# Reordering the first loads of a fused mixer kernel: modulation weights and projection weights ahead of x, two small vectors on another queue

## The chip, the cores and the metric

The kernel runs on one core of a Trainium2 chip. The metric is the device time of one execution in microseconds (us). The kernel before took 438.06 us, the median of three runs (437.89 to 438.6 us). Times inside an execution come from a hardware trace of one profiled execution; all of them are counted from the start of that execution's span.

The engines that appear below are PE (TensorE, matrix multiplications, with PEld for its weight loads), DVE (VectorE), ACT (ScalarE), POOL (GpSimd) and SP (SyncE, which here does nothing but issue DMA transfers).

## What is computed

One inference step of a mixer layer on 640 tokens of width 1024: 128 context tokens and 512 latent tokens. Each group has its own conditioning vector, from which a modulation (shift, scale, gate) is computed; both groups pass through the same weights. Cut to what matters here:

```python
mod   = silu(c) @ w_ada + b_ada              # (3*1024), once for context, once for latent
shift, scale, gate = split(mod, 3)
h     = rmsnorm(x, g_pre) * (1 + scale) + shift
proj  = h @ w_in                             # 1024 x 3840
qa, ka, va, ga, qr, zf, zb, ir, gr, uf, gf = split_columns(proj)
# three branches: neighbourhood attention, bidirectional gated recurrence, Fourier mixing,
# each multiplied by the SiLU of its gate columns
mixed = concat(oa * silu(ga), o_r * silu(gr), o_f * silu(gf))
y     = x + gate * rmsnorm(mixed @ w_out, g_post)
```

The modulated, normalised input h is needed by every projection, so nothing of the three branches can start before the first part of h is there. The outputs are y for both groups, the context keys and values, and the final recurrence states.

## The kernel before, in words

**Data layout.** The width of 1024 is cut into 8 row blocks of 128 (index k). h is kept transposed: for each k a 128x640 tile, feature on the partition, token along the row. Products that need more than the precision of one pass are split: a matrix is written as hi + lo (`hT_105`/`hT_106` for h, `hi`/`lo` for weights), and three passes hi·hi, lo·hi and hi·lo are added in PSUM (`mm3`).

**The start stage** (`start_stream`, `zf_stream`). The following happens for each k:

1. Two 512 KB blocks of modulation weights (`wss`, tiles named `vs` and `pT`) are multiplied with the silu of the conditioning vectors (`csil`): eight 32-column matmuls each (`mod_cols`). Here this is called modulation k, with halves a and b.
2. DVE copies the result from PSUM to `row`; four matmuls with the constant `sel` sum the partial rows (named sel k below); DVE makes G and shift for this k (lines 269 to 271 of the profile).
3. PE transposes the 128 columns of x that belong to k, one 128x128 block for each of the five token blocks i (`txa_107` to `txa_111` hold columns 0 to 639, `txb_112` to `txb_116` the rest), into PSUM. ACT applies G and shift while reading it (`modulated`, L235 for the four latent blocks, L237 for the context block), DVE writes the hi part (L238) and the lo part (L239) of hT.
4. The first projection (`zf`, two weight blocks zf0 and zf1, tiles `raw`, split by ACT into hi at L127 and by DVE into lo at L128) takes twelve 128x320 matmuls for each k, accumulated in four PSUM banks (`pb_117` to `pb_120`).

x itself comes as ten transfers (`load_x`), five token blocks of 320 KB + 192 KB. Before the transposes, `scale_x` takes for each token block the sum of squares (ACT Square at L223, DVE at L224), the reciprocal root (L161, L162, L226) and scales x in place (DVE, L228 and L229).

**What sets the order.** An object `Order` keeps a model clock `od.now` and lets several generators take turns by due times; the order in which they emit instructions is refined by a scheduler with its own timing. Each engine then executes its list in order and waits on semaphores. All large loads are issued by SP, one after the other in program order (`load_raw`, `load`); at most eight transfers are outstanding, since each new one reuses the completion semaphore of the eighth before it and waits for it. POOL issues three small loads (`bss`, `gpre`, `sel`). `cc` (8 KB, the conditioning vectors) and `lbl` (2 KB) are the first two transfers on SP's queue.

**After the start stage** come the other projection blocks (`block`), recurrences, attention, Fourier mixing and the output projection, all fed by weights that SP loads two blocks ahead into the two `raw` buffers.

Of the kernel before, what the change touches and what calls it, by code (L numbers as in the profile page):

```python
# [19 lines left out]
KT = 8  # L20
# [8 lines left out]
EARLY = 3  # L29
# [42 lines left out]
def mixer_kernel(ctx: ExitStack, tc: tile.TileContext, A, O):  # L72
    nc = tc.nc
    sc, ve, gp, te, sy = nc.scalar, nc.vector, nc.gpsimd, nc.tensor, nc.sync
# [8 lines left out]
    od = Order()  # L83
# [3 lines left out]
    def nm(s):  # L87
        n_[0] += 1
        return f"{s}_{n_[0]}"

    def T(cols=NT, dt=F32, tag=""):
        return tp.tile([P, NT], dt, tag="t", name=nm("t" + tag))[:, :cols]

    def PE_():
        return tp.tile([P, 512], F32, tag="pe", name=nm("pe"), bufs=WB["pe"])

    def S(cols):
        if cols <= 16:
            return sp.tile([P, 16], F32, tag="s", name=nm("s"))[:, :cols]
        return sp.tile([P, 320], F32, tag="m", name=nm("m"), bufs=WB["m"])[:, :cols]  # L100
# [4 lines left out]
    def PB(tag="b"):  # L105
        return ps.tile([P, 512], F32, tag=tag, name=nm("pb"), bufs=WB["p" + tag])
# [3 lines left out]
    def mm(out, lhsT, rhs, start=True, stop=True):  # L110
        n, m = rhs.free_size(), lhsT.free_size()
        od.now += 1e-3 * (n * 0.4167 * 4 if rhs.dtype == F32 else max(n * 0.4167, m * 0.83)) + 2e-3
        return te.matmul(out, lhsT, rhs, start=start, stop=stop).ins  # L113
# [8 lines left out]
    def tr(out, src):  # L122
        od.now += 0.107
        last_tr[0] = te.transpose(out, src, ident).ins  # L124

    def split(src, hi, lo, hi_eng=None, lo_eng=None):
        (sc.copy if hi_eng is None else hi_eng.tensor_copy)(hi, src)  # L127
        (ve if lo_eng is None else lo_eng).tensor_sub(lo, src, hi.bitcast(F32))  # L128
# [5 lines left out]
    def const(name, shape, dt=F32, dma=gp.dma_start):  # L134
        t = cp.tile([P, *shape], dt, tag=name, name=name)
        if name in A:
            dma(t, A[name])
        return t

    cc = const("cc", [KT, 2], dma=sy.dma_start)  # L140
    lbl = const("lbl", [2, 2], dma=sy.dma_start)
    bss = const("bss", [KT, 2])
    gpre = const("gpre", [KT])
    sel = const("sel", [2, P])
# [14 lines left out]
    def rsqrt_mean(ss, n):  # L159

        sc.activation(ss, ss, ACT.Sqrt, bias=eps, scale=1.0 / n)  # L161
        ve.reciprocal(ss, ss)  # L162
# [9 lines left out]
    def load_raw(src, tag, shape=(KT, P)):  # L172
        t = (tp if tag == "vs" else wp).tile([P, *shape], F32, tag=tag, name=nm(tag), bufs=WB[tag])
        with tc.issue_after(wdma[-1]) if wdma else ExitStack():
            wdma.append(sy.dma_start(t, src).ins)
        return t

    def split_w(raw, lo_eng=None, shape=(KT, P), tags=("hi", "lo")):
        hi, lo = [wp.tile([P, *shape], F32R, tag=t, name=nm(t), bufs=WB[t]) for t in tags]
        split(raw, hi, lo, lo_eng=lo_eng)  # L180
        return hi, lo
# [5 lines left out]
    def load(t, src):  # L187

        with tc.issue_after(wdma[-1]) if wdma else ExitStack():
            sy.dma_start(t, src)  # L190

    def mod_cols(out, w):

        t = od.now
        for k in range(KT):
            o = out[32 * (k % 4):32 * (k % 4) + 32, :]
            mm(o, csil[:, k, :], w[:, k, :], start=(k < 4), stop=(k >= 4))
        od.now = t + 0.45
# [5 lines left out]
    def xcols(i, k):  # L204
        return (xa[i] if k < 5 else xb[i])[:, k % 5 * P:k % 5 * P + P]
    zf_w, zf_acc = [], [[PB("f"), PB("f")], [PB("f"), PB()]]
# [8 lines left out]
    def load_x():  # L215
        for i in range(5):
            load(xa[i], A["x"][i * P:(i + 1) * P, 0:NT])
            load(xb[i], A["x"][i * P:(i + 1) * P, NT:D])

    def scale_x():  # L220
        for i in range(5):
            ss2 = S(2)
            sc.activation(T(), xa[i], ACT.Square, accum_out=ss2[:, 0:1])  # L223
            ve.tensor_tensor_reduce(PE_()[:, 0:384], xb[i], xb[i], 1.0, 0.0, op0=ALU.mult, op1=ALU.add,  # L224
                                    accum_out=ss2[:, 1:2])
            ve.tensor_add(rstd[:, i:i + 1], ss2[:, 0:1], ss2[:, 1:2])  # L226
            rsqrt_mean(rstd[:, i:i + 1], D)
            ve.tensor_scalar(xa[i], xa[i], rstd[:, i:i + 1], 0.0, op0=ALU.mult, op1=ALU.add)  # L228
            ve.tensor_scalar(xb[i], xb[i], rstd[:, i:i + 1], 0.0, op0=ALU.mult, op1=ALU.add)  # L229

    def modulated(k, pm):
        h, px = T(), PB()
        for i in range(1, 5):
            tr(px[:, (i - 1) * P:i * P], xcols(i, k))
        sc.activation(h[:, P:NT], px, ACT.Identity, bias=shift[:, k, 1:2], scale=G[:, k, 1:2])  # L235
        tr(pm[:, 384:512], xcols(0, k))
        sc.activation(h[:, 0:P], pm[:, 384:512], ACT.Identity, bias=shift[:, k, 0:1], scale=G[:, k, 0:1])  # L237
        ve.tensor_copy(hT[0][:, k, :], h)  # L238
        ve.tensor_sub(hT[1][:, k, :], h, hT[0][:, k, :].bitcast(F32))  # L239
        od.set(f"h{k}", LAT["h"])  # L240

    def start_stream():
        load_x()
        raws, zraw = [], []

        def loads(k):
            for u in range(2):
                raws.append(load_raw(A["wss"][2 * k + u], RAW[2 * k + u]))
            if k < 2:
                zraw.append(load_raw(A["win"][k], "raw"))  # L250

        for k in range(EARLY):
            loads(k)
        scale_x()
        od.now = 11.0
        for k in range(KT):
            if k + EARLY < KT:
                loads(k + EARLY)
            row = sp.tile([P, 256], F32, tag="AC", name=nm("row"), bufs=2)
            pm = PB()  # L260
            for u in range(2):
                mod_cols(pm[:, u * P:(u + 1) * P], raws[2 * k + u])
            yield 0
            ve.tensor_copy(row, pm[:, 0:256])
            yield LAT["row"]
            pt = pm[:, 256:260]
            for u in range(2):
                mm(pt[:, u * 2:u * 2 + 2], row[:, u * P:(u + 1) * P], sel[:, :, 0:1].rearrange("p a b -> p (a b)"))
            ve.tensor_scalar(G[:, k, :], pt[:, 0:2], bss[:, k, 0:1], 1.0, op0=ALU.add, op1=ALU.add)
            ve.tensor_scalar_mul(G[:, k, :], G[:, k, :], gpre[:, k:k + 1])  # L270
            ve.tensor_scalar_add(shift[:, k, :], pt[:, 2:4], bss[:, k, 1:2])
            modulated(k, pm)
            if k < 2:
                zf_w.append(split_w(zraw[k]))
            if k == 1:
                od.set("zw", 0.0)
            yield max(0.0, 13.5 + 2.7 * (k + 1) - od.now)

    def zf_stream():
        yield "zw"  # L280
# [9 lines left out]
        od.set("zf", 0.0)  # L290

    od.add(start_stream())
    od.add(zf_stream())

# [834 lines left out]
```

## Time and profile before

| | |
|---|---|
| time before, median of 3 runs | 438.06 us (437.89 to 438.6) |
| the profiled execution, its own time | 439.14 us |
| its span, first to last instruction | 437.3 us |
| PE busy in the span | 413.5 us, 95% |
| DVE / ACT busy | 302.3 us, 69% / 205.1 us, 47% |
| read from HBM / written | 43.80 MB / 3.28 MB |

The profile page gives the busy time of each engine, the span in 40 slices, and the chain of work that ended last, followed back from the last instruction to the first. The trace can be asked for instructions in order of time, for the same chain piece by piece, for the busy time of each engine in chosen windows, and for single tiles with the time from a DMA's issue to its landing. Matmul ends are modelled, so a busy PE is not always a PE at its peak rate; the distance from start to start is the better price.

### The profile page before, as it was taken

What the parts mean: (1) busy time and instruction counts of PE and PEld (TensorE: products, weight loads), DVE (VectorE), ACT (ScalarE), POOL (GpSimd) and SP (SyncE); (2) the same over time, 40 slices, a digit from 0 to 9 for tenths busy, and PEclk for the clock granted to TensorE, in tenths of its full rate; (3) what the DMA queues carried; (4) which work ended last, traced back from release to release, by engine and by line L of the source; (5) the groups of instructions that cost most, each with busy time, mean ns of one, the idle gap of its engine ahead of it and who ended that gap; (6) DMA issues with size and microseconds to landing.
All of it is one profiled execution on the core that took longest, in us unless ns stands there. A gap on an engine that the chain in (4) does not pass through costs nothing.

```text
span 437.3 us, 8333 instructions
## 1 busy us (share of the span) xinstructions
PE 413.5 (95%) x3192; PEld 375.1 (86%) x3192; DVE 302.3 (69%) x858; ACT 205.1 (47%) x546; POOL 7.4 (2%) x23
## 2 busy tenths in 40 slices
PE   0699999999998999999999999999999999999994
PEld 0488999999987998999899889989898988988884
DVE  2765478999987775885497748886768928670174
ACT  5533366566341525654454544743456643250151
POOL 2000000000020100000000000000000000000000
PEclk9999999999999999999999999999999999999999
DMA  7995144121211111132112413345134302481033
GB/s 243 412 407 216 48 117 150 50 72 49 59 49 46 37 64 48 55 97 58 47 54 73 146 48 103 98 135 161 61 120 146 98 0 65 140 276 61 0 119 124
DMA packets 19528, 47.62 MB, mean 109 GB/s; under 512 B 3184, under 2 KB 6912, under 8 KB 19488
## 3 DMA queue, kind: packets, MB, share of 16 engines
q1 hardware_dynamic: 19376, 46.94, 31.7%
q8 instruction: 25, 0.41, 0.4%
q0 software_dynamic: 112, 0.14, 0.2%
q14 instruction: 15, 0.12, 0.1%
HBM read 43.80 MB, written 3.28 MB: 108 GB/s over the span
## 4 chain that ended last, share of the span: by engine, by line
PE 91%; DVE 3%; DMA 3%; ACT 1%; issue 1%; SPq 0%; DVEq 0%; ACTq 0%
PE pb L113 85%; PE pb L124 6%; DMA vs<-wss 1%; DMA txa<-x 1%; DVE AL L448 1%; DVE t L522 1%; DVE AL L485 0%; ACT L677 0%; DVE t L951 0%; ACT pe L678 0%; DVE t L465 0%; DVE t L464 0%; DVE AC L448 0%; DVE t L466 0%; SPq L190 0%
## 5 line engine op out<-in xcount | busy, mean ns | idle before, releaser
L113 PE MATMUL pb<-hT,hi 128*128 128x320 f32 x896 | 209.0, 317 | 2.5 <-DVE vs L128 1.5
L113 PEld LDWEIGHTS pb<-hT,hi 128*128 128x128 f32 x896 | 148.9, 188 | 9.0 <-issue 3.3
L113 PE MATMUL pb<-hT,lo 128*128 128x320 f32 x448 | 139.2, 312 | 0.0
L113 PEld LDWEIGHTS pb<-hT,lo 128*128 128x128 f32 x448 | 84.0, 188 | 1.3 <-issue 0.2
L128 DVE TENSOR_TENSOR lo<-raw,hi 128x1024 fp32r<-128x1024 f32 x35 | 42.8, 1222 | 21.1 <-ACT hi L127 20.7
L127 ACT CAST hi<-raw 128x1024 fp32r<-128x1024 f32 x35 | 36.8, 1050 | 29.1 <-PE pb L113 17.5
L113 PE MATMUL pb<-t,t 64*128 64x128 f32 (+2 forms) x414 | 42.9, 291 | 0.4 <-DVE AL L448 0.4
L113 PEld LDWEIGHTS pb<-t,t 64*128 64x128 f32 (+1 forms) x414 | 36.0, 188 | 4.7 <-issue 0.7
L127 ACT CAST pT<-pb 128x256 fp32r<-128x256 f32 x64 | 23.4, 372 | 23.0 <-PE pb L124 11.4
L113 PE MATMUL pb<-hi,mh 128*128 128x512 f32 (+1 forms) x108 | 30.8, 376 | 0.0
L128 DVE TENSOR_TENSOR pT<-pb,pT 128x256 fp32r<-128x256 f32 x64 | 26.4, 417 | 1.7 <-ACT pT L127 1.5
L677 ACT ACTIVATE pe<-pb,s 128x256 f32<-128x256 f32 x32 | 15.2, 476 | 17.5 <-DVE s L676 8.5
L113 PEld LDWEIGHTS pb<-hi,mh 128*128 128x128 f32 x108 | 19.7, 188 | 3.8 <-DVE mh L128 0.3
L113 PE MATMUL pb<-pT,mh 128*128 128x512 f32 (+1 forms) x102 | 21.9, 364 | 0.0
L124 PE MATMUL pb<-ident,pe 128*128 128x128 f32 x136 | 21.0, 274 | 0.5 <-ACT pe L678 0.5
L113 PEld LDWEIGHTS pb<-pT,mh 128*128 128x128 f32 x102 | 17.7, 189 | 3.1
L113 PE MATMUL pb<-lo,mh 128*128 128x512 f32 (+1 forms) x54 | 19.5, 376 | 0.0
L932 ACT ACTIVATE t<-pb 128x512 f32<-128x512 f32 (+1 forms) x11 | 6.0, 552 | 27.3 <-PE pb L113 27.3
L688 DVE TENSOR_TENSOR o<-pb,o 64x512 f32<-64x512 f32 (+1 forms) x16 | 7.8, 486 | 15.5 <-ACT o L687 15.4
L124 PEld LDWEIGHTS pb<-ident,pe 128*128 128x128 f32 x136 | 16.5, 140 | 1.7 <-ACT pe L678 0.7
L448 DVE COPY_PREDICATED AL<-masks,pb 128x512 f32<-128x512 uint32 x24 | 16.5, 741 | 1.8 <-PE pb L113 1.8
L113 PE MATMUL pb<-pT,vs 128*128 128x256 f32 (+1 forms) x96 | 17.0, 320 | 0.0
(204 smaller groups left out, 636.3 us busy)
## 6 DMA issues: line engine op xcount, KB each, us to landing
raw<-win SPq DMA_DIRECT2D x30, 512.0 KB, 3.4
pT<-wss SPq DMA_DIRECT2D x12, 512.0 KB, 10.2
raw<-wg SPq DMA_DIRECT2D x8, 512.0 KB, 3.4
raw<-wout SPq DMA_DIRECT2D x8, 512.0 KB, 3.8
t<-x SPq DMA_DIRECT2D x10, 256.0 KB, 5.6
o_y<-t SPq DMA_DIRECT2D x9, 256.0 KB, 2.0
vs<-wss SPq DMA_DIRECT2D x4, 512.0 KB, 9.2
tbl<-tbl SPq DMA_DIRECT2D x4, 512.0 KB, 3.9
```

The lines of the kernel that those rows point to most:

```text
L113: return te.matmul(out, lhsT, rhs, start=start, stop=stop).ins
L124: last_tr[0] = te.transpose(out, src, ident).ins
L127: (sc.copy if hi_eng is None else hi_eng.tensor_copy)(hi, src)
L128: (ve if lo_eng is None else lo_eng).tensor_sub(lo, src, hi.bitcast(F32))
L448: ve.copy_predicated(out, mk.to_broadcast([P, i1 - i0, P]), src)
L522: ve.scalar_tensor_tensor(sall[r, cdst], sall[r, cs], Td[r, ip:ip + 1], pst[r, cdst], op0=ALU.mult, op1=ALU.add)
L677: sc.activation(pe[:, 256:512], ss[:, 256:512], ACT.Exp, bias=m[:, 1:2], accum_out=m[:, 3:4])
L688: ve.tensor_add(out, src[r, :], out)
L932: sc.activation(T(512)[:, cs], po[:, 0:cs.stop - cs.start], ACT.Square, accum_out=ssb[:, j:j + 1])
```

## The change

The two small vectors `cc` and `lbl` are now loaded by ScalarE's queue instead of SP's. In `start_stream` the loads are issued in another order: the two modulation blocks of k = 0, both zf weight blocks, the ten parts of x, and then the modulation blocks of k = 1, 2 and so on. Before, x came first, then the modulation blocks of k = 0, zf0, those of k = 1, zf1, and the rest.

The instructions follow: the two zf weight blocks are split before x is scaled, modulation 0 with its G and shift is computed ahead of `scale_x`, and the model clock is set to 5.0 instead of 11.0 and the due times of the following k from 13.5 to 14.5.

```diff
-    cc = const("cc", [KT, 2], dma=sy.dma_start)
-    lbl = const("lbl", [2, 2], dma=sy.dma_start)
+    cc = const("cc", [KT, 2], dma=sc.dma_start)
+    lbl = const("lbl", [2, 2], dma=sc.dma_start)
...
     def start_stream():
-        load_x()
+
         raws, zraw = [], []
 
         def loads(k):
             for u in range(2):
                 raws.append(load_raw(A["wss"][2 * k + u], RAW[2 * k + u]))
-            if k < 2:
-                zraw.append(load_raw(A["win"][k], "raw"))
-
-        for k in range(EARLY):
+
+        loads(0)
+        for p in range(2):
+            zraw.append(load_raw(A["win"][p], "raw"))
+        load_x()
+        for k in range(1, EARLY):
             loads(k)
-        scale_x()
-        od.now = 11.0
+        for p in range(2):
+            zf_w.append(split_w(zraw[p]))
+        od.set("zw", 0.0)
+        od.now = 5.0
         for k in range(KT):
...
             ve.tensor_scalar_add(shift[:, k, :], pt[:, 2:4], bss[:, k, 1:2])
+            if k == 0:
+                scale_x()
+                yield 10.0
             modulated(k, pm)
-            if k < 2:
-                zf_w.append(split_w(zraw[k]))
-            if k == 1:
-                od.set("zw", 0.0)
-            yield max(0.0, 13.5 + 2.7 * (k + 1) - od.now)
+            yield max(0.0, 14.5 + 2.7 * (k + 1) - od.now)
```

SP's queue at the very start. Before, in SP's list (cc and lbl are the small vectors, txa and txb the parts of x):

```order
L137 DMA cc<-cc 128x16
L137 DMA lbl<-lbl 128x4
L190 DMA txa_107<-x 128x640
L190 DMA txb_112<-x 128x384
L190 DMA txa_108<-x 128x640
L190 DMA txb_113<-x 128x384
```

In the changed kernel (vs_121 and pT_123 are the modulation weights of k = 0, raw_125 and raw_127 are zf0 and zf1):

```order
L175 DMA vs_121<-wss 128x1024
L175 DMA pT_123<-wss 128x1024
L175 DMA raw_125<-win 128x1024
L175 DMA raw_127<-win 128x1024
L190 DMA txa_107<-x 128x640
L190 DMA txb_112<-x 128x384
```

Four transfers of 512 KB now stand ahead of x, and the two small ones are gone from SP. From the loads of k = 2 on, SP's list is the same as before.

PE's list up to the first matmuls of the zf projection (`pb_117<-hT`). Before, from sel 0 on (vs_143 is the first half of k = 2):

```order
L113 MATMUL pb_202<-sel,row_201 128x2 x2
L113 MATMUL pb_247<-pT_137,csil 32x128 x8
L124 MATMUL pb_271<-ident,txa_108 128x128
L124 MATMUL pb_271<-ident,txa_109 128x128
L124 MATMUL pb_271<-ident,txa_110 128x128
L124 MATMUL pb_271<-ident,txa_111 128x128
L124 MATMUL pb_202<-ident,txa_107 128x128
L113 MATMUL pb_247<-pT_139,csil 32x128 x8
L113 MATMUL pb_117<-hT_105,hi_238 128x320
L113 MATMUL pb_118<-hT_105,hi_238 128x320
L113 MATMUL pb_119<-hT_105,hi_281 128x320
L113 MATMUL pb_296<-vs_143,csil 32x128 x8
```

In the changed kernel, from the last transposes of k = 1 on (pT_141 is the second half of k = 1, vs_143 the first half of k = 2, pb_314 the transposes of k = 2):

```order
L124 MATMUL pb_236<-ident,txa_111 128x128
L124 MATMUL pb_275<-ident,txa_111 128x128
L113 MATMUL pb_251<-pT_141,csil 32x128 x8
L113 MATMUL pb_290<-vs_143,csil 32x128 x8
L124 MATMUL pb_314<-ident,txa_108 128x128
L124 MATMUL pb_314<-ident,txa_109 128x128
L124 MATMUL pb_314<-ident,txa_110 128x128
L124 MATMUL pb_314<-ident,txa_111 128x128
L113 MATMUL pb_117<-hT_105,hi_147 128x320
L113 MATMUL pb_118<-hT_105,hi_147 128x320
L113 MATMUL pb_119<-hT_105,hi_151 128x320
L113 MATMUL pb_290<-pT_145,csil 32x128 x6
```

The first half of modulation 2 and four transposes of k = 2, which followed the first zf matmuls before, now stand ahead of them.

ACT's list at the start of the changed kernel (hi_147 and hi_151 are the zf weights; before, the list began with the table load of L152 and went from csil straight to L223, and the two casts came after the last L161):

```order
L137 DMA cc<-cc 128x16
L137 DMA lbl<-lbl 128x4
L168 ACT_TABLE_LOAD
L168 ACTIVATE csil<-cc 128x8x2
L152 ACT_TABLE_LOAD
L152 ACTIVATE lb<-lb 128x4
L127 CAST hi_147<-raw_125 128x1024
L127 CAST hi_151<-raw_127 128x1024
L223 ACTIVATE t_186,s_185<-txa_107 128x640
```

From the first matmul of the next projection block (zb0) on, the lists of all engines are the same instructions in the same order as before.

## Prediction

> **What bounds the kernel now.** I read the page first (span, slices, chain), then the first 49 us in windows, then the chain of that stretch piece by piece.
>
> ```profile
> span 437.3 us, 8333 instructions
> ...
> PE   0699999999998999999999999999999999999994
> ...
> PE 91%; DVE 3%; DMA 3%; ACT 1%; issue 1%; SPq 0%; DVEq 0%; ACTq 0%
> ```
>
> PE makes up 91% of the chain, and only the first two of 40 slices show a PE that is far from full. The windows (us, then busy us and instruction counts of PE, PEld, DVE, ACT, POOL, then clock, DMA share, GB/s) say how the start is divided:
>
> ```profile
> 0.00:14.20 14.20, 0.00 (x0) 0.02 (x1) 6.35 (x29) 9.05 (x19) 3.08 (x11) 1.00 0.85 283
> 14.20:22.04 7.84, 7.63 (x77) 4.96 (x77) 5.00 (x16) 3.15 (x5) 0.00 (x0) 1.00 1.03 410
> 22.04:29.02 6.98, 6.98 (x93) 5.49 (x93) 4.62 (x11) 1.59 (x3) 0.00 (x0) 1.00 1.03 407
> ```
>
> For 14.2 us PE does nothing; from 22 us it is full. The chain (start, length, what) names what fills the gap:
>
> ```profile
> 0.73 0.39 SPq L137
> ...
> 1.65 0.42 SPq L190
> ...
> 2.59 5.73 DMA txa<-x
> ...
> 8.34 5.74 DMA vs<-wss
> ...
> 14.21 1.08 PE pb L113 x16
> ...
> 17.21 0.44 DVE row L264
> ...
> 17.69 2.02 PE pb L113 x20
> ...
> 21.50 0.50 DVE hT L238
> ```
>
> First x is awaited, because the ninth and later transfers wait for earlier ones, then the modulation weights of k = 0, which SP could issue only at 8.34. Then modulation 0, sel 0, modulation 1 and transposes run one behind the other until hT exists at 22 us. After 50 us PE waits little for others; the longest such wait (total us, times, longest) is
>
> ```profile
> PE pb L113 <- DVE vs L128: 1.5, 1, 1.5
> ```
>
> So what PE gains at the start should reach the end almost whole, and the lists after zb0 are unchanged. I therefore follow PE to one marker with the same work behind it in both orders, the first zf matmul of k = 1, which starts the row at 29.05 here: by then modulations 0 to 3, sel 0 to 2, all zf of k = 0 and the same transposes are done.
>
> ```profile
> 18.63 1.08 PE L113 MATMUL pb<-pT,csil 128*32 128x128 f32 x16
> 19.64 1.33 PE L124 MATMUL pb<-ident,txa 128*128 128x128 f32 x5
> ...
> 20.90 1.08 PE L113 MATMUL pb<-pT,csil 128*32 128x128 f32 x16
> 22.04 1.12 PE L113 MATMUL pb<-hT,hi 128*128 128x320 f32 x3
> 23.10 0.64 PE L113 MATMUL pb<-vs,csil 128*32 128x128 f32 x16
> ...
> 28.63 0.66 PE L124 MATMUL pb<-ident,txa 128*128 128x128 f32 x4
> 29.05 0.97 PE L113 MATMUL pb<-hT,hi 128*128 128x320 f32 x5
> ...
> 31.00 0.51 PE L113 MATMUL pb<-sel,row 128*128 128x2 f32 x4
> 31.43 0.64 PE L113 MATMUL pb<-vs,csil 128*32 128x128 f32 x16
> 31.89 0.62 PE L113 MATMUL pb<-pT,csil 128*32 128x128 f32 x16
> ```
>
> Up to 21.98 a half modulation of 16 matmuls takes 1.01 us from start to start (18.63 to 19.64) and a transpose 0.25 (19.64 to 20.90 for five). Later they take 0.46 (31.43 to 31.89) and 0.10 (28.63 to 29.05 for four), and the row at 23.10 is the first of the short kind. PE works at half speed at first, though the clock column reads 1.00 in every window: that column does not show it.
>
> **The change, part by part.**
>
> *The stream of loads.* SP's first big transfer is issued at 0.73 instead of 1.65, after cc and lbl. Landings before: the first 512 KB (both parts of token block 0) at 5.89, the fifth unit of 512 KB (the end of x) at 6.1 + 6.7 = 12.8, the twelfth (first half of k = 2) at 12.3 + 9.5 = 21.8.
>
> ```profile
> 5.89 0.56 DVE L224 CUSTOM_DVE_ANT_0 pe<-txb 128x384 f32<-128x384 f32 x1 [1.59 <-DMA txb<-x]
> ...
> L190 SPq DMA_DIRECT2D txb<-x x1: 607/607/607, 6.1 to 6.1; - x1
> ...
> DMA to landing us min/median/max: 6.7/6.7/6.7
> ```
>
> ```profile
> L175 SPq DMA_DIRECT2D vs<-wss x1: 328/328/328, 12.3 to 12.3; - x1
> ...
> DMA to landing us min/median/max: 9.5/9.5/9.5
> ```
>
> The last seven units took 9.0 us, 1.29 each; the four between took 6.9, which is 1.74 more than 4 × 1.29. Part of that is seen in the windows of 1 us:
>
> ```profile
> 6.00:7.00 1.00, 0.00 (x0) 0.00 (x0) 0.46 (x2) 0.17 (x2) 0.00 (x0) 1.00 1.10 300
> 7.00:8.00 1.00, 0.00 (x0) 0.00 (x0) 0.00 (x0) 0.00 (x0) 0.23 (x1) 1.00 0.89 241
> ```
>
> Against 410 GB/s these two are short by 0.28 MB, 0.7 us. In the new order the same bytes stand ahead of the twelfth unit, and at that time the engines move weights (4 KB rows) instead of x (2.5 and 1.5 KB rows). Whether the slow stretch belongs to x's rows or to that moment, the trace does not say. Bounds: unit 1 lands at 5.89 − 0.92 = 5.0, unit n at 5.0 + 1.29 (n − 1), with nothing or all of the 1.74 on top. I take half, 0.9. Then x ends (unit 9) at 16.2 (15.3 to 17.1) instead of 12.8, and the first half of k = 1 (unit 10) is there at 17.5 (16.6 to 18.3), of k = 2 (unit 12) at 20.1 instead of 21.8.
>
> *The small vectors.* Two issues of about 0.4 us move to an ACT that has nothing to do then. csil waits for cc as before; it was ready at 4.8, ahead of the new unit 1.
>
> ```profile
> 4.60 0.22 ACT L168 ACTIVATE csil<-cc 128x16 f32<-128x16 f32 x1
> ```
>
> Cost nothing: modulation 0 then has until x's end at 16, and only a delay of cc by 8 us and more would be felt.
>
> *Modulation 0 and the weight splits.* Two half modulations at 1.01 and sel 0 at 1.0, about 3 us at half speed, leave the chain of 14.2 to 22.0 and run while x is on its way. The casts (1.03 us each, row below) and subtractions of zf0 and zf1 also move into that wait; their weights are units 3 and 4, there at 9.8 at the latest by the sum above, so both engines are through when most of x is still to come. The last block of x was scaled for the transposes at 16.35, 3.5 us after x's end:
>
> ```profile
> 15.80 0.55 DVE L228 TENSOR_SCALAR txa<-txa,rstd 128x640 f32<-128x640 f32 x1
> ```
>
> With the same 3.5 it is 19.7 now. Two transposes of that block stand ahead of the second half of modulation 1; PE reaches them at about 19.5 at half speed, so little is waited.
>
> *The burst on PE.* With x late, PE has no stretch of solid work until modulation 1 lands at s = 17.5. From there to the marker it has: six half modulations × 0.52 (the 0.46 and a little for the change of work), 15 transposes × 0.105, two sel × 0.43 (31.00 to 31.43), twelve zf × 0.147 (six in 0.88, below), in all 3.1 + 1.6 + 0.9 + 1.8 = 7.4 us at full speed. I add 0.3 for short waits. Before, the 7.0 us from 22.04 to the marker held 5.7 of work at these prices (four half modulations, nine transposes, two sel, twelve zf) and 1.3 beyond it; part of that was the late split of zf1 (until 22.39), which is now early.
>
> ```profile
> 29.86 0.31 PE L113 MATMUL pb<-hT,lo 128*128 128x320 f32 x1
> ...
> 30.74 0.31 PE L113 MATMUL pb<-hT,lo 128*128 128x320 f32 x1
> ```
>
> ```profile
> 21.36 1.03 ACT L127 CAST hi<-raw 128x1024 fp32r<-128x1024 f32 x1
> ```
>
> Full speed came between 21.98 and 23.10, which is 4.3 to 5.4 us after 17.69, the start of the last stretch without a longer gap, and 7.8 to 8.9 us after PE's first matmul. With L for this delay, half of L is lost: marker = s + 7.7 + L/2. With s = 17.5 and L = 4.85 that is 27.6, against 29.05: **1.4 us earlier**.
>
> Bounds: s = 16.6 and no half speed at all 24.3 (4.7 earlier); s = 18.3 and L = 8.9 30.5 (1.4 later). I take the middle, since the new burst resembles the stretch from 17.69: modulation, transposes, modulation, without a break.
>
> [...]
>
> *Later loads.* From k = 3 on the weights come earlier than PE wants them: the last of them, issued at 26.5, landed 10.1 later at 36.6 and was used at 43.96. PE, not the stream, sets that pace, so the shift stays.
>
> ```profile
> L175 SPq DMA_DIRECT2D pT<-wss x1: 328/328/328, 26.5 to 26.5; - x1
> ...
> DMA to landing us min/median/max: 10.1/10.1/10.1
> ...
> 43.96 0.65 PE L113 MATMUL pb<-pT,csil 128*32 128x128 f32 x16
> ```
>
> The sum: span 437.3 − 1.4 = 435.9, the execution 439.14 − 1.4 = 437.7; that execution stood 1.1 above the median, so the median becomes 438.06 − 1.4 = **436.7 us**.
>
> **The rivals.**
>
> *More is gained.* The slow stretch belongs to x's rows, s = 16.6, and full speed comes at the short end, L = 4.3: marker 26.45, 2.6 earlier, 435.5 us. For it: every window of weights alone runs at 400 GB/s or more. Against: x must still pass.
>
> *Nothing to be seen.* Only the 0.92 us of issue comes through, s = 18.3, L = 5.4: marker 28.7, 0.35 earlier, 437.7 us. For it: the bytes are the same, and x, which is needed first for hT, lands 3 to 4 us later. That the change does not do what it says belongs here. [...]
>
> *Slower.* PE stays at half speed as long as it did from its first matmul, L = 8.9, and the stream keeps its slow stretch, s = 18.3: marker 30.5, 1.4 later, 439.5 us. It decides from s + L/2 = 21.35 on; with s = 17.5 from L = 7.7. For it: the half-speed time of 7.8 to 8.9 us was seen. Against: before 17.69 that stretch held a wait for DVE, and sel, whose matmuls stream two columns; the new burst has neither before its zf matmuls begin.
>
> **How the numbers follow.** Forecast 0.45 (436.2 to 437.3), more 0.20, nothing 0.27, slower 0.08. A measurement of this kernel tells about 0.2%, 0.9 us, from no change. Faster by more: 0.20 + 0.39 of the forecast's 0.45 = 0.59; within: 0.06 + 0.27 = 0.33; slower: 0.08. The range 435.2 to 438.1 takes in the first three and leaves out the slower one and an almost warm PE.
>
> **What would show it.** The first matmul at about 5 us instead of 14.2, and then an almost empty PE to about 17; x's end at 16 to 17, the first zf matmul near 22, that of k = 1 at 27.6 instead of 29.05; half-speed modulations until 21 to 23. If hT's first cast comes later than PE's first transposes of k = 2, x is on the path after all and the burst's sum is wrong. If the marker moves and the end does not, a later wait took the gain.

## The result, and the profile after

The changed kernel took 441.11 us (median of 6 executions, 440.53 to 441.63), the kernel before, run beside it, 438.6 us (437.89 to 438.86). The ratio is 1.0059, with a 95% interval of 1.0046 to 1.0072: the change costs about 2.5 us, where 1.4 us were forecast as a gain. A second series gave 441.57 against 439.07 (ratio 1.0058, interval 1.004 to 1.0076). The two profiled executions stand closer together: 440.55 us after, 439.14 before.

Page of the changed kernel: span, PE in 40 slices, shares of the chain.

```profile
span 438.8 us, 8334 instructions
...
PE   2499999999998999999999999999999999999994
...
PE 90%; DVE 4%; DMA 2%; ACT 2%; issue 1%; DVEq 0%; ACTq 0%
```

The first slice shows that PE now does something early (a 2 where a 0 stood), but the second has fallen from 6 to 4. The windows below (us, length, then busy us and instruction counts of PE, PEld, DVE, ACT, POOL, clock, DMA share, GB/s) are cut at the same two times in both kernels. Before:

```profile
0.00:14.00 14.00, 0.00 (x0) 0.00 (x0) 6.15 (x29) 9.05 (x19) 3.08 (x11) 1.00 0.84 281
14.00:22.60 8.60, 8.18 (x79) 5.54 (x80) 5.76 (x16) 3.51 (x5) 0.00 (x0) 1.00 1.03 411
```

After:

```profile
0.00:14.00 14.00, 2.95 (x36) 2.31 (x36) 5.40 (x21) 8.15 (x12) 3.07 (x11) 1.00 0.90 323
14.00:22.60 8.60, 5.65 (x45) 3.33 (x49) 6.47 (x25) 4.35 (x12) 0.00 (x0) 1.00 1.03 408
```

By 22.6 us the old order had done 79 matmuls and the new one 36 + 45 = 81. PE began 8 us sooner, yet the first projection started 1.5 us later. PE in order of time (start, length, operation, count, and in brackets the idle time before it and what ended it) shows where the head start went:

```profile
6.27 1.08 PE L113 MATMUL pb<-vs,csil 128*32 128x128 f32 x16 [6.27 <-ACT csil L168]
...
9.25 1.01 PE L113 MATMUL pb<-sel,row 128*128 128x2 f32 x4 [1.04 <-DVE row L268]
14.60 0.47 PE L124 MATMUL pb<-ident,txa 128*128 128x128 f32 x1 [4.33 <-DVE txa L228]
15.93 0.47 PE L124 MATMUL pb<-ident,txa 128*128 128x128 f32 x1 [0.86 <-DVE txa L228]
17.48 0.47 PE L124 MATMUL pb<-ident,txa 128*128 128x128 f32 x1 [1.07 <-DVE txa L228]
17.88 0.65 PE L113 MATMUL pb<-pT,csil 128*32 128x128 f32 x6
18.95 0.47 PE L124 MATMUL pb<-ident,txa 128*128 128x128 f32 x1 [0.42 <-DVE txa L228]
...
21.61 1.08 PE L113 MATMUL pb<-pT,csil 128*32 128x128 f32 x16
22.46 0.78 PE L113 MATMUL pb<-vs,csil 128*32 128x128 f32 x16
...
23.58 0.69 PE L113 MATMUL pb<-hT,hi 128*128 128x320 f32 x3
...
29.88 0.83 PE L113 MATMUL pb<-hT,hi 128*128 128x320 f32 x4
```

Four times PE waits for a scaled block of x (L228), 6.7 us in all; the modulation matmuls keep the long form (1.08) until 22.46; the first zf matmul comes at 23.58 (before 22.04) and the prediction's marker, the first zf matmul of k = 1, at 29.88 (before 29.05). The chain of waits up to that point (start, length, what) tells why x is late:

```profile
0.73 3.91 DMA cc<-cc
...
4.65 6.64 DMA txa<-x
...
12.17 1.28 ACT L161
...
18.34 0.56 DVE txa L228
```

The second block of x lands at 11.3, the root's table load of 1.28 us (L161) comes only behind it, and then DVE scales one block every 1.0 to 1.5 us; the last one starts at 19.33, against 15.80 before. From about 47 us on the offset of PE against the kernel before is constant, 1.2 us at the 73rd matmul of zf's kind and 1.2 at the 601st; the profiled pair loses all of that in the start stage, and 0.3 us more between PE's last matmul and the end of the span. These 1.4 to 1.5 us are what the traces can account for; the other 1 us of the 2.5 lies between the profiled executions and the medians.

### The profile page after: what moved, and what is told of

The parts are those of the page before. It is cut to its first block, busy times and chain, and to the rows that moved or that the text cites. A ratio compares the mean times of both kernels' runs of the same rounds, so it can differ in the third digit from the quotient of the medians.

```text
span 438.8 us, 8334 instructions
## 1 busy us (share of the span) xinstructions
PE 415.0 (95%) x3192; PEld 376.0 (86%) x3192; DVE 302.0 (69%) x858; ACT 205.3 (47%) x546; POOL 7.4 (2%) x23
## 4 chain that ended last, share of the span: by engine, by line
PE 90%; DVE 4%; DMA 2%; ACT 2%; issue 1%; DVEq 0%; ACTq 0%
PE pb L113 84%; PE pb L124 6%; DMA txa<-x 2%; DMA cc<-cc 1%; DVE AL L451 1%; DVE t L525 1%; DVE txa L228 0%; DVE AL L488 0%; DVE pe L224 0%; ACT L680 0%; ACT L161 0%; DVE txb L229 0%; DVE t L954 0%; ACT pe L681 0%; DVE t L468 0%
## 5 line engine op out<-in xcount | busy, mean ns | idle before, releaser
L128 DVE TENSOR_TENSOR lo<-raw,hi 128x1024 fp32r<-128x1024 f32 x35 | 42.8, 1224 | 20.2 <-ACT hi L127 20.1
L127 ACT CAST hi<-raw 128x1024 fp32r<-128x1024 f32 x35 | 36.8, 1050 | 28.3 <-PE pb L113 17.5
L127 ACT CAST pT<-pb 128x256 fp32r<-128x256 f32 x64 | 23.4, 373 | 23.1 <-PE pb L124 11.6
```

## The experiments

All ran in five rounds, with the kernel before run beside them. Its medians were 438.9 (e1 to e4), 439.07 (e5 to e8), 439.03 (e9 to e11) and 438.94 us (e12). Each ratio is against it. "Offset" is how much later than in the profile of before a given matmul of zf's kind (hT against hi or lo) starts, counted from the first.

**e1: the small vectors back on SP, else as changed.**

```diff
-    cc = const("cc", [KT, 2], dma=sc.dma_start)
-    lbl = const("lbl", [2, 2], dma=sc.dma_start)
+    cc = const("cc", [KT, 2], dma=sy.dma_start)
+    lbl = const("lbl", [2, 2], dma=sy.dma_start)
```

> The changed kernel with cc and lbl back at the head of SP's queue; the new order of the large loads stays. In the changed kernel cc landed at 4.7 us (1.7 us after its issue in the kernel before, 4.0 here), csil was ready at 6.2 and the lbl chain ended at 8.9, ahead of the splits and of x's scaling in the queues of ACT and DVE. Theory A (the small transfers beside the big ones are what costs): csil at about 4.8 again, x's first sum of squares on DVE at about 10 instead of 11.4, the last block of x scaled 1 to 1.5 us earlier than 19.9, the end 1 to 2 us earlier than the changed kernel, so near 439.5. Theory B (x behind 2.1 MB of weights is what costs, the small ones are hidden): the loads start 0.9 us later and nothing else moves; within 0.5 us of the changed kernel's 441.1 or slower.

Measured: 441.59 us, ratio 1.0054 (1.0041 to 1.0067), the time of the changed kernel. PE in order of time, and one row of its waits:

```profile
23.09 1.08 PE L113 MATMUL pb<-vs,csil 128*32 128x128 f32 x16
...
24.85 0.69 PE L113 MATMUL pb<-hT,hi 128*128 128x320 f32 x3
```

```profile
PE pb L113 <- DVE hT L238: 0.9, 1, 0.9
```

Modulation 0 starts sooner (5.61 instead of 6.27), but the loads on SP come later, and with them x (its second block at 11.92 instead of 11.30); PE is at half speed until 24.8. The row of waits is one that neither original kernel has, near 52 us, where PE waits for hT of the last row block. In e1 it moved the offset from 1.0 (97th zf matmul) to 2.4 us (121st). Up to that wait e1 stands only 0.2 us better than the changed kernel (1.0 for 1.2), so by the profile moving the small vectors is not what costs the time; the medians alone could not say so, because the wait is in e1's. It comes with the order in which the scheduler then places the last transposes; e3, e6, e10 and e11 have it too, and it takes 1.4 to 1.6 us from each.

**e2: the small vectors on ACT's queue in the kernel before.**

```diff
-    cc = const("cc", [KT, 2], dma=sy.dma_start)
-    lbl = const("lbl", [2, 2], dma=sy.dma_start)
+    cc = const("cc", [KT, 2], dma=sc.dma_start)
+    lbl = const("lbl", [2, 2], dma=sc.dma_start)
```

> The kernel before with only cc and lbl moved to ScalarE's queue. Theory A: cc again lands late, at 4 to 4.7 us, and csil with it, but modulation 0 waits for its weights until 14.2 anyway and x's second block until 8.8; the late lbl chain holds DVE until about 8.9, so x's scaling loses nothing or little, and the stream gains up to 0.9 us: 437.6 to 438.8 against 438.6 of the kernel before. Theory B (nothing of the small transfers matters): exactly the 0.9 us earlier stream, 437.7.

Measured: 439.69 us (438.27 to 440.44; one more execution took 2257.81 and is not in the ratio), ratio 1.0011 (1.0 to 1.0022). The profiled execution was its shortest:

```profile
13.15 1.08 PE L113 MATMUL pb<-vs,csil 128*32 128x128 f32 x16 [13.15 <-DMA vs<-wss]
...
17.04 0.61 PE L113 MATMUL pb<-sel,row 128*128 128x2 f32 x4 [0.19 <-DVE row L264]
...
20.32 0.82 PE L113 MATMUL pb<-hT,hi 128*128 128x320 f32 x3 [0.83 <-DVE hT L238]
```

The stream does start earlier, and the first modulation comes 1.06 us sooner (13.15 for 14.21). Here PE was at full speed from 17.0 on (sel in 0.61; 1.01 in the profile of before, where the rise came after 22), and the offset is −2.0 us. The median shows none of the gain of up to 0.9 us that both theories allowed. Executions of one kernel differ by 2 to 3 us (before: 437.41 to 440.42 in all these series), and the profile shows a single one.

**e3: the changed kernel, with 12 extra 128x256 matmuls behind modulation 0,** into a bank that the first zf matmul starts anew; nothing uses their result.

```diff
+    def warm(n, src):
+        for _ in range(n):
+            te.matmul(zf_acc[0][0][:, 0:256], ident, src, start=True, stop=True)
...
             if k == 0:
+                warm(12, row)
                 scale_x()
```

> The changed kernel with 12 additional 128x256 matmuls on PE after modulation 0 (into a PSUM bank that is overwritten later), so that PE works from about 9 to 16 us. If half speed at the head of the burst is what costs (in the changed kernel until about 22.4, 4.5 us after the burst begins): modulation 1, its transposes and modulation 2 run at full speed, the first zf matmul comes about 1.5 us earlier than 23.6, the end 1 to 2 us earlier than 441.1. If the burst is bound by x's scaling (last block scaled at 19.9): transposes still wait for it, PE is at full speed but idle in between, and the gain is 0.5 us or less.

Measured: 439.08 us, ratio 1.0015 (0.9998 to 1.0032), 2 us less than the changed kernel although PE does more.

```profile
18.01 0.64 PE L113 MATMUL pb<-pT,csil 128*32 128x128 f32 x16
...
22.14 0.68 PE L113 MATMUL pb<-hT,hi 128*128 128x320 f32 x3
```

The second half of modulation 1 takes 0.64 at 18.01 where it was of the long form, and the first zf matmul comes at 22.14 instead of 23.58. PE is at full speed from 12.2 on here. Half speed at the head of the burst is a price of its own. At the 97th zf matmul the offset is −1.7 us, against +1.2 in the changed kernel, so 2.9 us were won; the wait near 52 us takes 1.45 back.

**e4 and e11: the kernel before with 14 (e4, shown) or 18 (e11) such matmuls at its start,** their result as unused as in e3.

```diff
+    def warm(n):
+        for _ in range(n):
+            te.matmul(zf_acc[0][0][:, 0:256], ident, csil.rearrange("p a b -> p (a b)"), start=True, stop=True)
...
+        warm(14)
```

> The kernel before with 14 additional 128x256 matmuls at the start of PE's list, so that PE works from about 5 to 14 us. If half speed costs what the trace suggests (from 14.2 to about 22.5 PE runs at half speed, 8 us with some 1 us of waits), modulations and transposes take half as long and hT 0 comes 2 to 3 us earlier than 22.0, unless the weights of k = 1 (landed 17.9 and 19.2) hold them: then 1 to 2 us. End at 435.5 to 437.5 against 438.6. If the chain there is one of transfers and of DVE and ACT, within 0.5 us of 438.6.

> As e4 (14 extra matmuls at the start of the kernel before, 439.92), but 18, so that they last until the first weights land at about 14.9 us and TensorE does not stand idle for 2.2 us. Theory H: full speed from 14.9 instead of 18.35 (e4) and 22.5 (the kernel before): against before 7.6/2 = 3.8 us less at most, cut to 1 to 2 us by the next wait (e4 already waited 0.55 us for the copy of the row at 21.5), so 437 to 438. Theory X: no gain over e4, 439 to 440.

Measured: e4 439.92 us, ratio 1.0021 (1.0007 to 1.0035); e11 442.1 us, ratio 1.0068 (1.0053 to 1.0083). Both are misses. In e4 the extra work ended at 12.7, and 2.17 us later PE was at half speed again, until 18.35. The first zf matmul came at 21.95, no more than 0.09 us sooner than before, and the offset is +0.1 from the 25th zf matmul on. Waits for `row` (0.55 us below, 0.29 at 30.98) took part of what full speed could have won; the rest was not separated.

```profile
14.88 1.08 PE L113 MATMUL pb<-vs,csil 128*32 128x128 f32 x16 [2.17 <-DMA vs<-wss]
...
18.89 0.64 PE L113 MATMUL pb<-pT,csil 128*32 128x128 f32 x16
...
21.49 0.61 PE L113 MATMUL pb<-sel,row 128*128 128x2 f32 x4 [0.55 <-DVE row L269]
```

In e11 that gap was closed and PE ran at full speed from 14.3, ahead of its data:

```profile
17.60 0.64 PE L113 MATMUL pb<-pT,csil 128*32 128x128 f32 x16 [1.33 <-DMA pT<-wss]
...
20.71 0.61 PE L113 MATMUL pb<-sel,row 128*128 128x2 f32 x4 [0.29 <-DVE row L269]
21.43 1.05 PE L113 MATMUL pb<-vs,csil 128*32 128x128 f32 x16
...
28.81 0.65 PE L113 MATMUL pb<-pT,csil 128*32 128x128 f32 x16
```

From 21.4 to 28.3 it was at half speed once more, 6.9 us in the middle of dense work. A faster PE met its next late input, and a stretch of half speed followed the idle time. The mean granted clock of single executions points the same way in e4: its one execution with 0.997 took 438.39 us, the six with 0.993 took 438.94 to 440.07, and the five with 0.988 or 0.989 took 440.28 to 441.22. In e2, too, five of eleven have 0.994 and took 439.56 to 440.44, so a stretch of half speed may hide a gain there; this was not tested. By estimate, 3.4 us (the half-speed stretch of e4) at a granted clock of 0.50 (e11's reading, in the last section) lower that mean by 0.004 (1.7 of 437 us).

**e5: the changed kernel, with x loaded ahead of the first projection's weights** (and these split after x is scaled).

```diff
         loads(0)
+        load_x()
         for p in range(2):
             zraw.append(load_raw(A["win"][p], "raw"))
-        load_x()
         for k in range(1, EARLY):
             loads(k)
-        for p in range(2):
-            zf_w.append(split_w(zraw[p]))
-        od.set("zw", 0.0)
         od.now = 5.0
...
                 scale_x()
+                for p in range(2):
+                    zf_w.append(split_w(zraw[p]))
+                od.set("zw", 0.0)
```

> The changed kernel with x loaded right behind the modulation weights of k = 0, ahead of the two zf weight blocks, and the zf splits placed behind x's scaling; everything else as changed. x then stands behind 1.05 MB instead of 2.1 MB. Theory B (x behind the weights is the path: its second block lands at 11.3, the first reciprocal comes at 13.8, the last block is scaled at 19.9 and PE waits for it): x and the whole scaling come 2 to 2.6 us earlier, the first zf matmul at about 21.5 to 22 instead of 23.6, the end 1.5 to 2.5 us earlier than the changed kernel, 438.7 to 439.7. Theory C (half speed of PE at the head of the burst is what costs): the burst starts with modulation 1, whose weights come at the same time as in the changed kernel; the end moves by less than 0.7 us.

Measured: 441.57 us, ratio 1.0059 (1.0039 to 1.008): nothing won. The first zf matmul came 2.8 us sooner, yet the modulations still ran at half speed:

```profile
20.79 0.90 PE L113 MATMUL pb<-hT,hi 128*128 128x320 f32 x2 [0.47 <-DVE hT L238]
21.62 1.08 PE L113 MATMUL pb<-pT,csil 128*32 128x128 f32 x16
...
24.76 0.65 PE L113 MATMUL pb<-vs,csil 128*32 128x128 f32 x16
```

So bringing x forward does not win the loss back by itself: with five short stretches of work between 12 and 18 us, each behind a wait of 0.5 to 1.8 us, PE did not reach full speed before 24.6.

**e6: e1 with the square root's table loaded early,** by a one-element Sqrt behind csil whose result nothing uses.

```diff
     sc.activation(csil[:, :, 0:2], cc, ACT.Silu)
+    early = S(1)
+    sc.activation(early, csil[:, 0, 0:1], ACT.Sqrt, bias=eps, scale=0.0)
```

> The kernel of experiment 1 (changed order of the large loads, cc and lbl on SP) with one more instruction: a one-element square root on ACT right after csil, so that ACT's table for it is loaded at about 5 to 6 us, in idle time, and not for 1.28 us between the second token block's sum of squares and the first root. Theory B: that table load lies on the path of x's scaling, so the first scaling comes 1.2 us earlier than 14.6, and the end about 1.2 us earlier than experiment 1's 441.6, near 440.4. Theory C: DVE's scaling is earlier, but PE's burst is bound by its half speed and by modulation 1: 0.4 us or less.

Measured: 440.03 us, ratio 1.0026 (1.0014 to 1.0039), 1.5 us less than e1. The marker moves from 30.27 to 29.02, by about the table's length. Of these 1.25 us, 0.9 are there while PE is at half speed in both runs (second half of modulation 1, 1.08 long, at 21.35 for 22.23); the rest comes with full speed that is there 1.7 us earlier (23.1 for 24.8). The wait near 52 us is in both:

```profile
53.23 1.27 PE L113 MATMUL pb<-hT,hi 128*128 128x320 f32 x6 [0.93 <-DVE hT L240]
```

The table load was on the path of x's scaling, as the chain above shows. The prediction had taken over the length of that scaling, 3.5 us, from before unchanged.

**e7: e5, e1 and e6 together** (x ahead of the first projection's weights, small vectors on SP, table early).

> Experiments 5, 1 and 6 together: modulation weights of k = 0, x, zf weights; cc and lbl on SP; the early root. Theory B: x's second block lands near 9.5, the first scaling at about 10.5 to 11 as in the kernel before, the last block at 16.5 to 17; modulation 0 is done by 9; hT 0 then waits for x's transposes and comes at about 19.5 to 20 against 22.0 before; the end 1 to 2.5 us earlier than the kernel before, 436.5 to 438, if PE is at full speed by 21. Theory C: the same work is done earlier at half speed, PE rises later in its burst, and the end is within 1 us of the kernel before.

Measured: 440.08 us, ratio 1.003 (1.0015 to 1.0044). All that DVE and ACT need is early now (first zf matmul at 20.08), but modulation 1 still ran at half speed from 17.86 until after 21, and no gain over e6 is left:

```profile
21.18 0.80 PE L113 MATMUL pb<-pT,csil 128*32 128x128 f32 x16
```

**e8: the changed kernel again,** in the series of e5 to e7.

> The changed kernel once more, beside the three others on the same chip: 441.1 with 0.6 us to either side, and a profile in which the first zf matmul stands near 23.6; it shows how much of the differences is the time at which PE comes to full speed, which differed from run to run.

Measured: 441.57 us, as above; its profile repeats the first within 0.2 us (first zf matmul at 23.71).

**e9: e7 with the 12 extra matmuls of e3.**

> Theory H (half speed at the head of the burst is a cost of its own, added to that of x's scaling): the order of e7 (x ahead of the first projection's weights, small vectors on SP, square-root table early) took 440.08; its TensorE ran at half speed from 17.86 to about 21.5 us. With 12 extra 128x256 matmuls after modulation 0 it comes to its burst at full speed: 3.6/2 = 1.8 us less, so about 438.3, under the kernel before (438.9 to 439.1). Theory X (what is ready late sets the time, and the clock only fills gaps): the modulation weights of k=1 still land at 17.9 and hT at 20.0, so it stays at 440.

Measured: **436.92 us** (436.76 to 437.61), ratio 0.9949 (0.9937 to 0.9962): 2.1 us under the kernel before and more than 4 under the changed one.

```profile
10.62 7.86 PE L246 MATMUL pb<-row,ident 128*128 128x256 f32 x24
18.32 0.71 PE L124 MATMUL pb<-ident,txa 128*128 128x128 f32 x5
18.96 0.64 PE L113 MATMUL pb<-pT,csil 128*32 128x128 f32 x16
...
20.69 1.01 PE L113 MATMUL pb<-hT,hi 128*128 128x320 f32 x4
```

The profile shows no wait of PE between 10.6 us and the end of the start stage, and full speed from 15.5 on. The offset is −2.2 us at the 121st zf matmul and stays so. Against e7, which lacks only the extra matmuls, this is 3.2 us less, where 1.8 were expected; e7's profile, a short execution (439.0), shows 2.1 of them.

**e10 and e12: e6 with 12 or 15 extra matmuls** (the edit of e3, and 15 for 12).

> Theory H: e6 (small vectors on SP, square-root table early) took 440.03; its burst ran at half speed from 18.11 to about 23.2 us. The 12 extra matmuls take that away: up to 2.5 us less, of which the wait for x's last scaled block (scaled at 19.7) gives back about 0.7, so about 438.2. Theory X: the last block of x sets the first projection, and 440 stays. Both: the wait of 0.93 us for hT near 52 us, which e1, e3 and e6 have and the kernel before has not, is there again.

> e10 with 15 extra matmuls in place of 12. In e10 TensorE was at full speed at 17.1, stood idle for 0.94, 0.20 and 0.55 us between 17.75 and 20.9, and was at half speed again from 21.31 to about 24.8 us, a stretch that cost some 1.7 us. Theory H (idle time inside the burst costs a later stretch of half speed, in steps of about 3.4 us): three matmuls more last until about 18.6 and take the gap of 0.94 us away; the fallback does not come and the time is 438.6 to 439.2 (440.5 less 1.7, plus a few tenths for the later transposes). Theory R (the fallback comes by chance, whatever the gaps): it comes back in this run as in e10, and the time is 440.5 to 441.

Measured: e10 440.5 us, ratio 1.0026 (1.0006 to 1.0046); e12 439.1 us, ratio 1.0008 (0.9992 to 1.0023). The time of e10 is the one that theory X gave, but the profile shows another reason: PE came to full speed as theory H said and fell back after gaps of 0.94, 0.20 and 0.55 us:

```profile
18.44 0.33 PE L124 MATMUL pb<-ident,txa 128*128 128x128 f32 x1 [0.94 <-DVE txa L230]
...
20.91 0.47 PE L124 MATMUL pb<-ident,txa 128*128 128x128 f32 x2 [0.55 <-DVE txa L230]
...
22.16 1.08 PE L113 MATMUL pb<-vs,csil 128*32 128x128 f32 x16
```

In the profiled execution of e12 the first gap is filled, two of 0.55 are left, and no fallback follows:

```profile
20.52 0.44 PE L124 MATMUL pb<-ident,txa 128*128 128x128 f32 x2 [0.55 <-DVE txa L230]
...
22.61 0.64 PE L113 MATMUL pb<-vs,csil 128*32 128x128 f32 x16
```

The time falls by 1.4 us, as theory H said, but that does not prove H. The two profiled executions are 2.3 us apart: at the 97th zf matmul e12 is 0.87 us ahead, and the other 1.4 are the wait near 52 us, which e12 turned out not to have. And the profiled execution is one of e12's short ones: six of the twelve have a mean granted clock of 0.996 to 0.998 and took 438.15 to 438.78 us, the other six have 0.993 or 0.994 and took 439.42 to 440.42, as if the fallback had come in these. Whether the gap or chance decides (theory R) stays open.

## Why the prediction was wrong

*What held.* The first large loads moved as forecast: x ended at 15.9 (16.2 forecast), the first half of modulation 1 was there at 17.2 (s = 17.5), that of modulation 2 at 19.7 (20.1). PE's burst began at 17.48, though with a transpose that had waited for x, and full speed came 5.2 us later (4.85), near 22.7 (21 to 23). So half speed at the head of the burst was in the forecast, at nearly its right length. The first matmul came at 6.27 instead of 5, because cc took 3.91 us to land and a table load of 1.28 us came behind it; e1, where it came at 5.61, stood only 0.2 us better by the 97th zf matmul. The gap before 17 us was there, and zf's weights were split in it.

*The work of the burst: the largest error that the trace shows.* The sum had 7.4 us of matmuls at full speed and "0.3 for short waits". The counts were right but for one transpose: 96 modulation matmuls (six halves), two sel, twelve zf and 16 transposes (15 in the sum) ran between 17.48 and the marker. But of these about 5.4 us by the forecast's prices were left at 22.7, and they took 7.18 us to 29.88. The prediction had seen the same in the kernel before (7.0 us for 5.7 of work) and put part of the 1.3 down to the late split of zf1. The split is early now, and the excess is 1.75. With 1.3 in place of 0.3 the same sum gives a marker at 28.6 and a gain of 0.4 us only. The profile shows no wait of PE in this stretch. The rows place the excess where PE changes from one kind of matmul to the next, 14 times in the stretch, as here in the changed kernel:

```profile
28.10 0.61 PE L113 MATMUL pb<-sel,row 128*128 128x2 f32 x4
28.63 0.42 PE L113 MATMUL pb<-pT,csil 128*32 128x128 f32 x6
28.98 0.56 PE L113 MATMUL pb<-hT,hi 128*128 128x320 f32 x2
```

Six modulation matmuls need 0.17 us at 0.46 for sixteen, and the next kind begins 0.35 us after the first of them. This is read from the rows; no run varies the changes of kind alone. Of the 2.3 us by which the marker was missed (29.88 for 27.6), 1.45 are this term.

*Half speed and x.* The formula lost L/2 = 2.4 us there. In the 5.2 us from 17.48 PE did 2.4 half modulations and seven transposes, 2.0 us of work at full speed, so 3.2 were lost: the other 0.8 us of the miss. "So little is waited" for x's last block failed: its scaling ended as forecast (19.9 for 19.7), but PE waited for four blocks in turn, for one of them inside the burst (0.42 us before 18.95). How the rest of the 0.8 divides was not separated. The sign named for this, hT's first cast later than PE's transposes of k = 2, did not appear (22.31 against 23.17); it asked about the wrong place. What showed x on the path was PE's own waits for L228.

*From the marker to the end.* The shift did not stay as it was: the profiled offset grew from 0.84 at the marker to 1.2 at 47 us, and the end added 0.3. Between the marker and the 73rd zf matmul both kernels do the same matmuls (60 zf, 128 modulation, 20 sel, 21 transposes); PE changes from one kind to another 31 times there, 23 times before, and takes 18.55 us for 18.20. Together 0.85 + 0.35 + 0.3 = 1.5 us in the span, and 2.85 above the forecast of 437.7 for a profiled execution. The remaining 1.6 us of the miss (441.11 for 436.7) are no part of any trace: the step of 1.1 from the profiled execution to the median rested on three executions, and later series put the kernel before 0.5 to 1 us higher, while the changed kernel's two profiled executions are at or near the shortest of their series. That PE comes to full speed later in the longer ones would fit e2, whose shortest execution is the profiled one with full speed from 17.0 us on, but it is not shown.

*The rivals.* "Slower" gave 439.5 by staying at half speed for 8.9 us with a slow stream. Its marker, 30.5, was close by luck; its mechanism did not occur (5.2 us, loads as forecast). "Nothing" had the right reason, that x is needed first for hT and lands 3 us later, and too small a price. What neither the forecast nor a rival had priced is the two terms above, the work that took longer than its sum and the wait for x inside the burst.

The formula counts half speed afresh from the burst's start, as if the work in the early wait were not there, and had that right: the 36 matmuls of modulation 0 and sel 0, from 6.27 to 10.26 us, were done at half speed (1.08 us for a row of 16, 1.01 for sel), as the same ones had been before, and PE came to its burst at half speed again (1.08 at 21.61). The "almost warm PE" that the range left out, one with next to no half speed in its burst, did not occur. In the rows of extra matmuls below, PE came to full speed after 2.9 to 5.9 us without a wait. What ends half speed, and what brings it back, is not shown: a stretch of it followed a gap of 2.17 us in e4, gaps of 0.94, 0.20 and 0.55 in e10 and of 1.33 and 0.29 in e11, and none followed gaps of 0.52, 0.34 and 0.55 in e3's profile (0.65 for a row of 16 at 20.72) or two of 0.55 in e12's.

*What is shown and what is not.* Shown: half speed in the start stage costs time (e3, 2.0 us under the changed kernel; e9, 3.2 under e7), and so does x's scaling with its table load (e6, 1.5 under e1). The queue of the small vectors is not it (e2, and the profile of e1). The two prices overlap, since both fill the same wait; how the 2.5 us divide between them was not separated. The changes of kind, the largest term of the miss at the marker, are read from the rows and not tested.

## What to carry to other kernels

Work that is moved into an early wait leaves the path only if what then ends the wait is not later than before; here x, which a chain of table load, roots and scaling still had to follow, was pushed back by 3 us to make room for weights that were not urgent. Undoing that paid only together with an early table load and extra matmuls ahead of the burst (e9, 436.92 us), not alone (e5, 441.57). Look at the whole chain behind a transfer that is pushed back, at the work rate on both sides of the gap that it leaves, and when a stretch of the old profile took longer than its sum, do not explain the excess away by one event in it. In e11 PE lost more after two gaps between its matmuls than in the gaps themselves: 1.33 and 0.29 us of waiting were followed by 6.9 us at half speed, 3.4 us lost; that the gaps brought it is not shown. Filling idle time with extra matmuls paid most where all later inputs were there in time (e9, 3.2 us under e7), and cost time where they were not (e11, 442.1 us for 439.03 before).

## What the runs showed of the hardware that was not expected

PE's rate in a steady row of 128x256 matmuls doubled about 2.9 us after its start in e3 and e11, 3.3 in e4, 5.0 to 5.1 in e9 and e12, and 5.9 in e10. These are estimates from the lengths and counts of the rows (e10: 22 parts, two to a matmul, in 7.89 us; e11: 36 in 9.52), at 0.43 us from start to start of the parts at first and 0.22 later; the record of one part is 0.79 to 0.80 us at the longest and 0.38 at the shortest in both. Windows of two microseconds, cut to these matmuls alone (PE busy, with the count, and the granted clock behind PEld), of e11, which began at 4.84:

```profile
5.00:7.00 2.00, 2.00 (x5) 1.64 (x6) 1.00 1.04 314
...
9.00:11.00 2.00, 2.00 (x11) 1.75 (x10) 1.00 1.05 408
```

and of e10, which began at 8.51:

```profile
13.00:15.00 2.00, 2.00 (x8) 1.64 (x7) 1.00 1.05 388
```

The granted clock reads 1.00 in each of them, at either rate. So the column does not show half speed before the first rise, as the prediction said. It does show the later stretch of e11 (PE alone):

```profile
21.60:28.20 6.60, 6.33 (x49) 0.50 1.01 403
```

The half-speed stretches inside a burst lasted 3.4 us in e4 and e10 (14.9 to 18.3, 21.2 to 24.6) and 6.9 us, twice that, in e11. The mean granted clock of e11's six executions is 0.988 to 0.992; that of the changed kernel, at half speed until 22.46, is 0.996 to 0.998. So the mean was lower with such a stretch, and the first half speed does not show in it.

An 8 KB transfer on ACT's queue beside four of 512 KB on SP's took 3.7 to 3.9 us to land (after, e8), where 1.7 had been enough at the head of SP's queue.
